# Sharing a pair's moves between ScalarE and GpSimd, and reordering 39 transfers into 30, in a matmul with scale and add

## The chip, the cores and the metric

The kernel runs on one NeuronCore of one Trainium2 chip; the other cores are idle. PE is TensorE (the matmul engine), DVE is VectorE, ACT is ScalarE, POOL is GpSimd and SP is SyncE, which here only issues transfers. SBUF is the memory on the chip that the engines and transfers work on. The metric is the device time of one execution in microseconds (us), median of several; a profiled execution gives the trace. The span of the trace, from the first to the last instruction, is about 1.8 us shorter than the device time.

## The reference

```python
# x: 16 x 512 x 1024, weight: 1024 x 768, add_value: 16 x 512 x 768, all fp32; scale = 0.1
return (scale * np.matmul(x, weight) + add_value).astype(np.float32)
```

The 16 x 512 rows are 64 tiles of 128 rows. Whatever the kernel does, it must read x (33.6 MB), the addend (25.2 MB) and the weight (3.1 MB), and write 25.2 MB: 87.0 MB.

## The kernel before

All transfers are issued by SyncE (SP) in the order of one list. An entry is (what, first tile, number of tiles): x, w for weight, a for addend, o for output, l and r for the two column parts of the last output.

```python
STREAM = [
    ("x", 0, 3), ("w", 0, 2), ("w", 2, 2), ("w", 4, 2), ("x", 3, 1), ("w", 6, 2),
    ("a", 0, 3), ("x", 4, 4), ("a", 3, 1), ("a", 4, 4), ("x", 8, 4), ("x", 12, 4),
    ("x", 16, 4), ("a", 8, 8), ("x", 20, 4), ("x", 24, 8), ("o", 0, 8), ("a", 16, 8),
    ("x", 32, 8), ("a", 24, 8), ("a", 32, 8), ("x", 40, 8), ("o", 8, 8), ("x", 48, 8),
    # ... (15 more, down to)
    ("o", 62, 1), ("l", 63, 1), ("r", 63, 1),
]
X_SLOTS = 16      # x tiles held in SBUF
A_SLOTS = 32      # addend tiles; the output is written over them
MOVED_ACT = [14, 18, 22, ...]     # pairs of tiles moved by ScalarE
MOVED_POOL = [16, 20, 24, ...]    # pairs moved by GpSimd
```

PE needs x transposed and in bf16. The first 14 tiles (and the last four) are cast whole and transposed by PE. The others go in pairs: 16 casting copies of 32 partitions move blocks of a pair from x into a buffer, then VectorE turns 32 x 32 blocks with one stream transpose.

```python
    def move_pair(t0, a):                       # a quarter of the pair's 16 copies
        act = t0 in MOVED_ACT
        # ... (at a == 0: a buffer from a pool of two for ScalarE, of two for GpSimd)
        for b in range(4):
            move = nc.scalar.copy if act else nc.gpsimd.tensor_copy
            move(moved[t0][32 * b:32 * b + 32, :, a, :], src[32 * a:32 * a + 32, :, b, :])

    def turn_moved(t0):
        # ...
        nc.vector.transpose(xt..., moved.pop(t0)...)      # frees the buffer

    def step():                                 # one tile of 128 rows
        t = done["step"]
        for j in range(KJ):                     # 8 parts of K
            if j == KJ // 2:
                # ... transpose(t + 1) on PE if it is no moved tile; casts ahead
                for a in range(4):
                    if in_pair.get(t + 8 - a) == t + 8 - a:
                        move_pair(t + 8 - a, a)
            product(t, j, BOTH)                 # 128x512 and 128x256 matmuls, bf16
        finish(t, BOTH[0], 0, N)                # VectorE: product * scale + addend, over the addend
        if in_pair.get(t + 4) == t + 4:
            turn_moved(t + 4)
```

An x transfer may be issued when the tiles that it overwrites have been cast or moved; an addend transfer when the output that stood there has left; an output transfer when its tiles are finished. Three product buffers (PSUM) stand between PE and VectorE.

## Time and profile before

| | before |
|---|---|
| device time, median of 3 | 210.12 us (210.09 to 210.5) |
| span of the trace | 208.5 us |
| bytes on the one data queue | 87.03 MB, 5,616 packets |
| DMA share from 4 to 204 us | about 1.00, at 428 GB/s |
| PE, ScalarE, GpSimd, VectorE busy | 181.6, 129.0, 124.3, 101.3 us |

The rows are read against each other: no engine is busy all the time, while the 16 DMA rings (one queue, one ring on each of 16 DMA engines) are. The prediction below shows the lines. In a line of a stretch of time, each engine's busy us stands with the number of its instructions in brackets; then come the granted PE clock (1.00 is full), the DMA share and the GB/s moved. The share counts the time in which packets are under way. A transfer ends with 16 landings, one for each ring. The trace records when each came. In the kernel before, the 16 landings of a transfer lie within 0.4 us until 28 us and within 2.4 us at the end.

### The profile page before, as it was taken

The numbers are of one execution on the slowest core, as the hardware profiler recorded it, in microseconds if no ns is written. First come the engines' busy times: TensorE is split into PE (matmuls) and PEld (weight loads), VectorE is DVE, ScalarE is ACT, GpSimd is POOL, SyncE is SP. The second block draws the span as 40 slices with busy tenths as digits, with TensorE's granted clock in tenths as the row PEclk, the third lists the DMA queues.
The fourth block names the chain that finished last, engine by engine and source line by source line (L and its number), as shares of the span: only waits on it lengthen the run. The fifth ranks groups of instructions, "written<-read, shape, count | busy, mean of one in ns | idle before, by whom it ended". The sixth has DMA issues, their size and how long they took to land.

```text
span 208.5 us, 2886 instructions
## 1 busy us (share of the span) xinstructions
PE 181.6 (87%) x1096; PEld 110.7 (53%) x1096; DVE 101.3 (49%) x111; ACT 129.0 (62%) x206; POOL 124.3 (60%) x199
## 2 busy tenths in 40 slices
PE   0599399980899997999999999999999999989960
PEld 0455256650466664566666666666666666656630
DVE  0536535511466514855655555555553685233330
ACT  2423000499959798599999999999999900003210
POOL 1310524379898980999998899999999960001000
PEclk9999889996589999999999999999999999999997
DMA  6999999999999999999999999999999999999995
GB/s 236 415 428 440 413 429 434 421 450 406 454 418 448 407 429 462 404 443 420 442 434 413 461 418 424 420 429 437 421 434 424 432 439 424 429 418 439 429 394 214
DMA packets 5629, 87.21 MB, mean 418 GB/s; under 512 B 624, under 2 KB 752, under 8 KB 2032
## 3 DMA queue, kind: packets, MB, share of 16 engines
q1 hardware_dynamic: 5616, 87.03, 98.2%
q8 instruction: 8, 0.13, 0.3%
q14 instruction: 5, 0.04, 0.0%
HBM read 61.87 MB, written 25.17 MB: 417 GB/s over the span
## 4 chain that ended last, share of the span: by engine, by line
DMA 75%; ACT 9%; PE 7%; DVE 3%; SPq 1%; issue 1%; DVEq 0%
DMA out_dram<-ao 35%; DMA ao<-in_add_value_dram 22%; DMA xs<-in_x_dram 13%; ACT va L118 9%; PE mm L177 6%; DMA ao<-in_weight_dram 5%; DVE ao L185 2%; DVE xt L126 1%; PE tp L156 1%; SPq L258 1%; SPq L99 0%; SPq L264 0%; SPq L272 0%; DVEq L185 0%
## 5 line engine op out<-in xcount | busy, mean ns | idle before, releaser
L177 PE MATMUL mm<-w_bf,xt 128*128 128x256 bf16 (+1 forms) x1024 | 173.8, 331 | 8.8 <-DVE xt L164 6.6
L177 PEld LDWEIGHTS <-xt 128*128 128x128 bf16 x1024 | 101.3, 99 | 76.9 <-DVE xt L164 7.0
L118 ACT CAST va<-xs 32x512 bf16<-32x512 f32 x192 | 118.2, 616 | 28.8 <-DMA xs<-in_x_dram 19.1
L118 POOL CAST va<-xs 32x512 bf16<-32x512 f32 x176 | 106.8, 607 | 15.9 <-DVE xt L126 6.2
L185 DVE SCALAR_TENSOR_TENSOR ao<-mm,ao 128x768 f32<-128x768 f32 (+2 forms) x62 | 58.1, 942 | 78.1 <-PE mm L177 49.1
L146 POOL CAST xb<-xs 128x1024 bf16<-128x1024 f32 x15 | 15.2, 1040 | 43.4 <-PE tp L156 22.5
L164 ACT COPY xt<-tp 128x512 bf16<-128x512 bf16 (+1 forms) x11 | 8.2, 785 | 35.3 <-PE tp L156 35.3
L126 DVE STREAM_TRANSPOSE xt<-va 128x1024 f32<-128x1024 f32 x23 | 28.4, 1234 | 0.0
L156 PE MATMUL tp<-identity,xb 128*128 128x128 f32 x72 | 12.9, 314 | 11.2 <-DVE xb L142 7.4
L156 PEld LDWEIGHTS tp<-identity,xb 128*128 128x128 f32 x72 | 9.8, 161 | 13.7 <-issue 7.6
L164 DVE COPY xt<-tp 128x1024 bf16<-128x1024 bf16 x10 | 6.9, 686 | 10.1 <-PE tp L156 10.1
L101 DVE CAST w_bf<-ao 128x768 bf16<-128x768 f32 x8 | 4.1, 556 | 3.8 <-DMA ao<-in_weight_dram 3.8
L142 DVE CAST xb<-xs 128x512 bf16<-128x512 f32 x3 | 1.9, 696 | 6.8 <-DMA xs<-in_x_dram 6.8
L144 POOL CAST xb<-xs 128x512 bf16<-128x512 f32 x2 | 1.6, 834 | 5.5 <-DMA xs<-in_x_dram 5.5
L144 ACT CAST xb<-xs 128x512 bf16<-128x512 f32 x1 | 0.6, 618 | 4.8 <-DMA xs<-in_x_dram 4.8
L213 DVE TENSOR_SCALAR ao<-mm 128x768 f32<-128x768 f32 x2 | 1.8, 952 | 1.9 <-PE mm L177 1.9
L245 DVE TENSOR_TENSOR ao<-ao 128x768 f32<-128x768 f32 x3 | 2.7, 951 | 0.0
L144 ACT ACT_TABLE_LOAD x1 | 1.3, 1283 | 0.7 <-PEq L289 0.7
L210 ACT ACTIVATE ao<-mm 128x768 f32<-128x768 f32 x1 | 0.8, 817 | 0.0
masks.py:197 POOL MEMSET identity<- 128x128 f32 x1 | 0.2, 204 | 0.3 <-POOLq L289 0.3
masks.py:199 POOL TENSOR_SCALAR_AFFINE_SELECT identity<-identity 128x128 f32<-128x128 f32 x1 | 0.3, 292 | 0.1
L289 POOL MEMSET const-float32-0.0<- 128x1 f32 x1 | 0.1, 98 | 0.2 <-issue 0.2
(3 smaller groups left out, 0.3 us busy)
## 6 DMA issues: line engine op xcount, KB each, us to landing
ao<-in_add_value_dram SPq DMA_DIRECT2D x7, 3072.0 KB, 26.1
out_dram<-ao SPq DMA_DIRECT2D x7, 3072.0 KB, 23.9
xs<-in_x_dram SPq DMA_DIRECT2D x5, 4096.0 KB, 18.8
xs<-in_x_dram SPq DMA_DIRECT2D x5, 2048.0 KB, 26.6
ao<-in_weight_dram SPq DMA_DIRECT2D x4, 768.0 KB, 9.6
xs<-in_x_dram SPq DMA_DIRECT2D x1, 1536.0 KB, 6.1
ao<-in_add_value_dram SPq DMA_DIRECT2D x1, 1536.0 KB, 19.3
out_dram<-ao SPq DMA_DIRECT2D x1, 1536.0 KB, 12.9
```

What stands on the lines that cost most here:

```text
L101: nc.vector.tensor_copy(w_bf[:, j + i, :], ao[:, s + i, :])
L118: move(moved[t0][32 * b:32 * b + 32, :, a, :], src[32 * a:32 * a + 32, :, b, :])
L126: nc.vector.transpose(xt.rearrange("p i c m -> p (i c m)"), moved.pop(t0).bitcast(fp32).rearrange("p c a k -> p (c a k)"))
L142: nc.vector.tensor_copy(xb[:, 0:K // 2], src[:, 0:K // 2])
L144: other(xb[:, K // 2:K], src[:, K // 2:K])
L146: nc.gpsimd.tensor_copy(xb, src)
L156: nc.tensor.transpose(tp[:, c, :], pairs[:, c * P:(c + 1) * P], identity)
L164: evacuate(xt_tiles[t][:, c:c + q, :].bitcast(bf16), tp[:, c:c + q, :].bitcast(bf16))
L177: nc.tensor.matmul(mm_tiles[t, cols[0]][:, n0:n1], lhs(t, j), w_bf[:, j, n0:n1], start=(j == 0), stop=(j == KJ - 1))
L185: nc.vector.scalar_tensor_tensor(a, mm_tiles[t, part][:, n0:n1], float(scale), a, op0=mybir.AluOpType.mult, op1=mybir.AluOpType.add)
L245: nc.vector.tensor_add(ao[:, t, :], ao[:, EARLY_AT + t, :], ao[:, t, :])
L258: nc.sync.dma_start(xs[:, k:k + n, :], rows(x_v, s, n))
```

## The change

The intent: each pair's 16 copies are shared by two engines, so that a pair is ready in half the time; one pool of three buffers serves all pairs; the pairs reach to the last tile; and the transfers become fewer, larger and issued earlier. Cut to its core:

```diff
-    ("x", 0, 3), ("w", 0, 2), ("w", 2, 2), ("w", 4, 2), ("x", 3, 1), ("w", 6, 2),
-    ... 33 more
+    ("x", 0, 3), ("w", 0, 2), ("w", 2, 2), ("x", 3, 1), ("w", 4, 4), ("a", 0, 8),
+    ("x", 4, 4), ("x", 8, 8), ("a", 8, 8), ("x", 16, 8), ("a", 16, 8), ("x", 24, 8),
+    ("a", 24, 8), ("o", 0, 8), ("x", 32, 8), ("o", 8, 8), ("a", 32, 8), ("x", 40, 8),
+    ("o", 16, 8), ("a", 40, 8), ("x", 48, 8), ("o", 24, 8), ("a", 48, 8), ("x", 56, 8),
+    ("o", 32, 8), ("a", 56, 8), ("o", 40, 8), ("o", 48, 8), ("o", 56, 5), ("o", 61, 3),
...
-MOVED_ACT = [14, 18, 22, ..., 58]
-MOVED_POOL = [16, 20, 24, ..., 56]
+MOVED = [14, 16, 18, 20, ..., 60, 62]
...
-    va_pool = ctx.enter_context(tc.tile_pool(name="va_pool", bufs=2))
-    vp_pool = ctx.enter_context(tc.tile_pool(name="vp_pool", bufs=2))
+    va_pool = ctx.enter_context(tc.tile_pool(name="va_pool", bufs=3))
...
         for b in range(4):
-            move = nc.scalar.copy if act else nc.gpsimd.tensor_copy
-            move(moved[t0][32 * b:32 * b + 32, :, a, :], src[32 * a:32 * a + 32, :, b, :])
+            for a, move in ((2 * half, nc.scalar.copy), (2 * half + 1, nc.gpsimd.tensor_copy)):
+                move(moved[t0][32 * b:32 * b + 32, :, a, :],
+                     src[32 * a:32 * a + 32, :, b, :])
...
-                    for a in range(4):
-                        if in_pair.get(t + 8 - a) == t + 8 - a:
-                            move_pair(t + 8 - a, a)
+                    for half in range(2):
+                        if in_pair.get(t + 6 - half) == t + 6 - half:
+                            move_pair(t + 6 - half, half)
```

## The prediction

> **What bounds the kernel now.** I read the page's part 1 first, then part 2, then part 3, then the chain of waits and the stretches at both ends. Part 1 alone would suggest TensorE:
>
> ```profile
> PE 181.6 (87%) x1096; PEld 110.7 (53%) x1096; DVE 101.3 (49%) x111; ACT 129.0 (62%) x206; POOL 124.3 (60%) x199
> ```
>
> Part 2 and part 3 say otherwise:
>
> ```profile
> PE   0599399980899997999999999999999999989960
> ...
> PEclk9999889996589999999999999999999999999997
> DMA  6999999999999999999999999999999999999995
> ...
> DMA packets 5629, 87.21 MB, mean 418 GB/s; under 512 B 624, under 2 KB 752, under 8 KB 2032
> ...
> q1 hardware_dynamic: 5616, 87.03, 98.2%
> ```
>
> The reader is to see that PE has holes (the 0 at slice 10, the 3 and 8 before it) while the DMA row is 9 in every slice but the first and the last. All transfers leave one queue, and its packets fill 98.2% of 16 engines' time: 0.982 x 208.5 = 204.7 us. The chain of waits agrees, 75% DMA:
>
> ```profile
> DMA 75%; ACT 9%; PE 7%; DVE 3%; SPq 1%; issue 1%; DVEq 0%
> ```
>
> The other 25% looks like an invitation to speed up ScalarE, and the waits of the issuing queue do too: its x transfers waited 90.1 us for ScalarE's moves, once for 22.0 us. But a late issue costs only if the queue behind it ran empty. In stretches of 20 us it never did:
>
> ```profile
> core 0: us, PE busy (x) PEld busy (x) DVE busy (x) ACT busy (x) POOL busy (x), PEclk, DMA share, GB/s
> ...
> 44.00:64.00 20.00, 13.43 (x71) 8.12 (x70) 6.92 (x9) 17.59 (x30) 18.03 (x30) 0.74 1.00 428
> ...
> 104.00:124.00 20.00, 20.00 (x125) 12.02 (x123) 11.47 (x12) 19.60 (x33) 18.09 (x30) 1.00 1.01 432
> ```
>
> The first of these holds the worst wait (the x issue at 49.1 us) and a PE idle for some 6 us with a reduced clock, and still the DMA share is 1.00 at 428 GB/s. I check it by counting bytes. An x tile is 0.524 MB; a tile of addend, output or weight is 0.393 MB. By the stream's order 22.02 MB had been issued before that transfer. From 4 to 204 us the rate is 428 GB/s ((87.21 - 0.73 - 0.82) MB in 200 us, the two ends taken from their own stretches), and 0.73 MB had moved by 4 us, so a byte at position B leaves at about 2.3 + B/0.428 us. At 49.1 us some 20 MB were gone: 2 MB, or 4.7 us, were still queued. The tightest wait in the old kernel was hidden, with little to spare.
>
> What is not full is a start of 2.3 us and the end, where the data thin out as the 16 rings finish one after another. Compute ended at 202.04 us, the data at about 207.5 us:
>
> ```profile
> 202.00:204.00 2.00, 0.00 (x0) 0.00 (x0) 0.05 (x1) 0.00 (x0) 0.00 (x0) 1.00 0.96 391
> 204.00:206.00 2.00, 0.00 (x0) 0.00 (x0) 0.00 (x0) 0.00 (x0) 0.00 (x0) 0.90 0.87 342
> 206.00:208.00 2.00, 0.00 (x0) 0.00 (x0) 0.00 (x0) 0.00 (x0) 0.00 (x0) 0.50 0.18 66
> ```
>
> **What the Trainium skill says.** "DMA: Bandwidth & Descriptors", section "Where 436 GB/s comes from", gives 435.2 GB/s as the ceiling of the 16 ports. The trace's 428 to 432 GB/s in full stretches is within 2%, so there is no rate left to win. Its section "Why small descriptors are slow (HBM only)" says that every packet carries a fixed overhead. The packet records of this trace agree that there is one: the median packet took 46 ns for 1,024 B and 1,213 ns for 32,768 B, which is 8.4 ns plus 0.0368 ns a byte; 24,576 B took 912 ns, as that line says. "TensorE: Matmul & The Clock Gate", Part 1, says that an idle window of about 3.4 us halves the PE clock. The trace agrees: PE idle 21.1 to 24.5 us is followed by a clock of 0.50 (26 to 28 us), while the idle 1.2 us near 81 us leaves it at 1.00.
>
> **The change part by part.**
>
> 1. Bytes: none removed. 87.03 MB go through the same queue and rings, 203.3 us at 428 GB/s.
>
> 2. Transfers: 39 become 30. The counts fit one packet per partition row of a transfer and 16 semaphore packets for each transfer: 39 x 144 = 5,616, as part 3 has it. After: 30 x 128, plus 128 because the weight half has two rows a partition, plus 30 x 16 = 4,448. 1,168 packets less at 8.4 ns on 16 rings are 0.6 us. Doing it by size with the medians (before 128 x 46, 128 x 84, 512 x 122, 128 x 159, 512 x 234, 128 x 352, 384 x 461, 640 x 614, 1,792 x 912, 640 x 1,213, semaphores 624 x 9; after 128 x 159, 512 x 234, 128 x 352, 128 x 461, 128 x 574, 128 x 614, 1,920 x 912, 896 x 1,213, 480 x 9) gives 203.2 and 202.4 us of each ring. **Gain on the path: 0.7 us.** It is the only term that I can find there.
>
> 3. The moves. Before, a pair's 16 casts run on one engine: 16 x 0.626 = 10.0 us on ScalarE from first to last, two pairs side by side. After, 8 on each engine: 5.0 us a pair, pairs one after another. Throughput is the same, 2.5 us a tile; latency halves. There are 25 pairs for 23: ScalarE 200 x 0.616 = 123 us, GpSimd 200 x 0.607 plus 11 whole casts of 1.04 and two halves of 0.83, about 134.5 us, both under 203 us. PE loses four tiles' transposes (4 x 0.44 = 1.8 us on its last chain), ScalarE four evacuations of 1.01 us, VectorE gains two transposes of 1.23 us. All of it lies beside the transfers: worth 0.
>
> 4. Issue earlier. Positions in the new queue over 0.428, plus 2.3: x 24-31 starts at 61 us and may be issued when pair 14 is moved and tile 13 is cast, about 51 us; x 32-39 starts at 85 us and needs pair 22 moved, about 75 us (x 16-23 lands near 55 us, then four pairs of 5 us); x 40-47 starts at 110 us, issued at 95; x 48-55 starts at 134 us, issued near 117. Margins of 10 to 17 us in place of under 5. But nothing was lost before, so this saves nothing.
>
> 5. The start. The whole addend 0-7 now stands ahead of x 4-7, which lands near 28 us in place of 23.4. PE idles some 8 us there and restarts at half clock. PE's own work is about 176 us and the addend's arrivals hold it up again later, so this delay is absorbed.
>
> 6. The end. Addend 56-63 has 77.59 MB up to its end in both orders, so it lands as before, near 185.6 us. PE then has tiles 59 to 63 to do (three product buffers, 56 to 58 computed already): 186.7 + 5 x 2.60 = 199.7, last VectorE write about 200.3 us, against 202.04. The last transfer (three tiles) can be issued at 200.4 us and its data begin about 1 us later (the first issue at 0.74 us had data before 2.0 us). The queue reaches it at 2.3 + 85.85/0.428 = 202.9 us. It is hidden by about 1 us.
>
> Sum: 210.1 - 0.7 = **209.4 us**.
>
> **The rivals.** (a) *The earlier issue pays*: if stalls of the issuing queue were real gaps, several us would return, and the 90 us of waits for ScalarE and the 7% of PE in the chain speak for it. Against it is a DMA share of 1.00 in those very stretches. To be over 2% faster, 206 us, the rings would have to move 87 MB at over 434 GB/s; I give it almost nothing. (b) *The last output is exposed*: one transfer of 1.18 MB waits for the last tile where there were five small ones. With PE late by 2 to 3 us (a stall of over 3 us before tile 48, 56 or 59 would halve its clock for some us; I count stalls of 1.4 to 2.6 us there), the margin of 1 us is gone and the time is 210.5 to 212 us. For it: x 56-63 comes 36 us before the end of the data, in place of 51. Against it: moves take half as long, and PE has 1.8 us less to do. (c) *ScalarE and GpSimd in lockstep become the bound*, since each pair now needs both: they give a pair every 5.0 us where PE needs 5.2 us for two tiles. A tie that shows as small PE waits, not as time. (d) *The fewer packets are worth nothing*, because the slowest ring sets the end: the last transfers' landings in the trace spread over 2.4 us between first and last ring. Then 210.1 us stays. The packets taken away are spread evenly over the rings, so I count on most of the 0.7.
>
> **Range and chances.** Expected 209.4. Low, 208.7: packets pay in full, and larger rows close the end more sharply (the last 4 us moved 0.25 MB less than a full rate). High, 210.4: rival (d) plus a little of (b). Faster by over 2% 0.02, within 2% 0.95, slower by over 2% 0.03, which would need a ring run dry or PE half-clocked near the end.
>
> **What would show it right or wrong.** Right: DMA row 9 throughout, the queue's packets 4,448 and about 204 us of ring time, 428 to 432 GB/s in full stretches, waits of x issues for ScalarE or GpSimd still there but no dip after them, the last addend landing near 185.6 us, the last VectorE write near 200, and the span shorter by 0.5 to 1 us. Wrong: a stretch with DMA share well under 1 in the middle (a refused issue), or a last write after 202 us followed by a dip before the last output. The prediction would fail most easily at step 6.

## The result, and the profile after

The changed kernel took **210.1 us** (median of 4, 210.01 to 210.2), the kernel before 210.28 us in the same rounds (median of 4). The ratio is **0.9991** with a 95% interval of 0.9974 to 1.0009. Two later measurements of the same changed kernel gave 1.0011 and 1.0009. There is no change that can be told from noise, where 0.7 us (ratio 0.9967) had been predicted.

The page of the changed kernel, lines that answer to those shown in the prediction:

```profile
PE 177.1 (85%) x1059; PEld 108.4 (52%) x1080; DVE 104.1 (50%) x113; ACT 129.9 (62%) x210; POOL 135.2 (65%) x219
...
PE   0498339999999999999999999999959996799930
...
DMA  6999999999999999999999999999999999999994
...
DMA packets 4461, 87.21 MB, mean 418 GB/s; under 512 B 480, under 2 KB 480, under 8 KB 1120
...
q1 hardware_dynamic: 4448, 87.03, 97.9%
...
DMA 44%; PE 38%; POOL 10%; SPq 1%; issue 1%; DVE 1%; POOLq 0%; DVEq 0%
```

The packets are the 4,448 that were counted beforehand, the rings' time is 0.979 x 208.4 = 204.0 us (before 204.7), and the DMA row has no hole. The chain of waits has changed its face, 38% PE where it was 7%, and the time has not: the chain follows what released each step last, and with a full queue many paths end together. The DMA row, with the GB/s, decides which of them costs.

The issues of four x transfers in the timeline of the changed kernel (start, duration, what):

```profile
54.59 0.33 SPq L250 DMA_DIRECT2D xs<-in_x_dram  x1
...
76.98 0.33 SPq L250 DMA_DIRECT2D xs<-in_x_dram  x1
...
97.91 0.33 SPq L250 DMA_DIRECT2D xs<-in_x_dram  x1
...
118.84 0.33 SPq L250 DMA_DIRECT2D xs<-in_x_dram  x1
```

By the prediction's formula the queue reaches these transfers at 61, 85, 110 and 134 us, so they stood in it 6 to 15 us ahead. The margin is real, and it bought nothing.

The stretches at the end of the changed kernel, with the columns as before:

```profile
202.00:204.00 2.00, 0.00 (x0) 0.00 (x0) 0.00 (x0) 0.00 (x0) 0.00 (x0) 0.95 0.94 401
204.00:206.00 2.00, 0.00 (x0) 0.00 (x0) 0.00 (x0) 0.00 (x0) 0.00 (x0) 0.50 0.68 286
206.00:208.00 2.00, 0.00 (x0) 0.00 (x0) 0.00 (x0) 0.00 (x0) 0.00 (x0) 0.50 0.08 32
```

and VectorE in its timeline, where the fields after the operation are what it waited for:

```profile
185.65 0.96 DVE L178 SCALAR_TENSOR_TENSOR ao<-mm,ao 128x768 f32<-128x768 f32 x1 [2.19 <-DMA ao<-in_add_value_dram]
...
199.86 0.42 DVE L178 SCALAR_TENSOR_TENSOR ao<-mm,ao 128x256 f32<-128x256 f32 x1 [0.18 <-PE mm L170]
```

The last addend is used at 185.65 us as predicted (185.67 before), and the last write ends at 200.28 us (202.04 before). Fewer bytes are left after 204 us than in the kernel before (286 and 32 GB/s in the last two stretches where it had 342 and 66), so most rings do finish sooner. The execution does not.

**The rings.** The landing records of the trace tell why. The table gives, for two transfers that end at the same number of bytes in all of these kernels (output 48 to 55, and the last one), the first ring, the mean and the slowest, in us from the first instruction; the last column is the device time of the same profiled execution. e0, e1 and e11 are repeats; e2, e3 and e4 are told below.

| run | output 48-55: first, mean, slowest | last: first, mean, slowest | device time |
|---|---|---|---|
| before | 197.69, 198.97, 200.12 | 205.17, 206.41, 207.59 | 210.28 |
| before (e0) | 197.96, 199.15, 200.38 | 205.44, 206.62, 207.85 | 210.54 |
| changed | 197.34, 198.76, 200.19 | 204.61, 206.03, 207.46 | 210.20 |
| changed (e1) | 197.52, 198.90, 200.58 | 204.81, 206.19, 207.87 | 210.62 |
| changed (e11) | 197.24, 198.74, 200.16 | 205.56, 206.23, 207.45 | 210.19 |
| e2, packets doubled | 198.83, 200.13, 201.57 | 206.23, 207.51, 208.96 | 211.59 |
| e3, 2 of 8 products | 197.26, 198.10, 200.63 | 204.53, 205.37, 207.92 | 210.67 |
| e4, 1 of 8 products | 197.34, 198.16, 200.68 | 204.65, 205.45, 207.96 | 210.72 |

Two things are to be read. The device time is the slowest landing plus 2.6 to 2.8 us in every row. And the mean ring gains 0.4 us from the change (206.03 against 206.41; 206.19 against 206.62 in the second pair), while the slowest ring gains 0.13 us in one pair and loses 0.02 us in the other. Two traces of one kernel differ in the mean by 0.16 to 0.21 us, so the 0.4 us is clear of that, though not by much. The gain is there, on rings that nobody waits for.

### The profile page after: what moved, and what is told of

Its sections match the earlier page's. It is cut to its first block, busy times and chain, and to the rows that moved or that the text cites. A ratio compares the mean times of both kernels' runs of the same rounds, so it can differ in the third digit from the quotient of the medians.

```text
span 208.4 us, 2843 instructions
## 1 busy us (share of the span) xinstructions
PE 177.1 (85%) x1059; PEld 108.4 (52%) x1080; DVE 104.1 (50%) x113; ACT 129.9 (62%) x210; POOL 135.2 (65%) x219
## 3 DMA queue, kind: packets, MB, share of 16 engines
q1 hardware_dynamic: 4448, 87.03, 97.9%
## 4 chain that ended last, share of the span: by engine, by line
DMA 44%; PE 38%; POOL 10%; SPq 1%; issue 1%; DVE 1%; POOLq 0%; DVEq 0%
PE mm L170 36%; DMA out_dram<-ao 17%; DMA ao<-in_add_value_dram 15%; DMA xs<-in_x_dram 12%; POOL va L110 9%; PE tp L149 2%; DVE ao L178 1%; SPq L93 1%; SPq L250 1%; POOL xb L139 1%; SPq L256 0%; POOLq L139 0%; DVEq L178 0%
## 5 line engine op out<-in xcount | busy, mean ns | idle before, releaser
L170 PE MATMUL mm<-w_bf,xt 128*128 128x512 bf16 (+1 forms) x1003 | 170.6, 327 | 8.3 <-DVE ao L178 6.0
L110 ACT CAST va<-xs 32x512 bf16<-32x512 f32 x200 | 123.2, 616 | 46.0 <-DMA xs<-in_x_dram 43.5
L110 POOL CAST va<-xs 32x512 bf16<-32x512 f32 x200 | 121.7, 608 | 20.8 <-DMA xs<-in_x_dram 11.9
L178 DVE SCALAR_TENSOR_TENSOR ao<-mm,ao 128x768 f32<-128x768 f32 (+2 forms) x62 | 57.2, 935 | 40.3 <-PE mm L170 34.0
L119 DVE STREAM_TRANSPOSE xt<-va 128x1024 f32<-128x1024 f32 x25 | 31.1, 1244 | 29.5 <-POOL va L110 29.0
L139 POOL CAST xb<-xs 128x1024 bf16<-128x1024 f32 x11 | 11.2, 1043 | 29.4 <-DMA xs<-in_x_dram 21.8
L149 PE MATMUL tp<-identity,xb 128*128 128x128 f32 x56 | 10.2, 317 | 14.5 <-DVE xb L135 7.7
L149 PEld LDWEIGHTS tp<-identity,xb 128*128 128x128 f32 x56 | 7.7, 163 | 16.4 <-issue 7.7
L157 ACT COPY xt<-tp 128x512 bf16<-128x512 bf16 (+1 forms) x7 | 4.1, 655 | 9.2 <-PE tp L149 9.2
```

Source lines behind the costliest of these rows:

```text
L119: nc.vector.transpose(xt.rearrange("p i c m -> p (i c m)"), moved.pop(t0).bitcast(fp32).rearrange("p c a k -> p (c a k)"))
L139: nc.gpsimd.tensor_copy(xb, src)
L149: nc.tensor.transpose(tp[:, c, :], pairs[:, c * P:(c + 1) * P], identity)
L157: evacuate(xt_tiles[t][:, c:c + q, :].bitcast(bf16), tp[:, c:c + q, :].bitcast(bf16))
L170: nc.tensor.matmul(mm_tiles[t, cols[0]][:, n0:n1], lhs(t, j), w_bf[:, j, n0:n1], start=(j == 0), stop=(j == KJ - 1))
L178: nc.vector.scalar_tensor_tensor(a, mm_tiles[t, part][:, n0:n1], float(scale), a, op0=mybir.AluOpType.mult, op1=mybir.AluOpType.add)
```

## The experiments

My theory after the result: each packet costs less than its record shows, and of what is gained the slowest ring gets little, because the rings drift apart during the run. The rivals: the packets are free; or compute at the end sets the time after all; or the two halves of the change, moves and list, each have an effect and cancel. Thirteen runs were made, three of them repeats (e0, e1, e11). Each is compared with the kernel before on the same chip in the same rounds.

### e0 and e1: both kernels again

No edit.

> The kernel before, unchanged, timed against itself: what two timings of one program differ by, and a second trace. Both theories: 210.2 us, ratio 1.000. The ring theory (instruction fetches delay single rings, and the slowest ring sets the end): the 16 landings of the last transfer spread over 2.2 to 2.7 us again, with the first jump at the first 16 KB instruction packet. If the spread were chance it would differ by over 0.5 us.

> The changed kernel, unchanged, for a tighter interval and a second trace. Ring theory: the packets saved show in the mean landing of the last transfer (0.4 to 0.7 us under the kernel before), the slowest ring eats a part; 209.9 to 210.1 us, ratio 0.998 to 0.9995. Rival (the packets taken away cost nothing on the rings): mean landing as before, ratio 1.000.

Measured: e0 210.12 us, ratio 0.9995 (0.9979 to 1.0012); e1 210.5 us, ratio 1.0011 (0.9997 to 1.0025). One program differs from itself by about as much as the change does. Of e1's expectation the mean landing came (0.43 us sooner) and the ratio under 0.9995 did not. The spread of the last landings was 2.4 us again in e0 and 3.1 us in e1. In all four traces of the two kernels so far the first wide jump follows the first 16 KB packet of the instruction queue (before: packet at 30.3 us, spread 0.38 us until the transfer that landed at 28 us, 1.71 us in the next).

### e2: the same bytes in twice as many packets

```diff
-            nc.sync.dma_start(xs[:, k:k + n, :], rows(x_v, s, n))
+            for d, e in halves(n):            # (0, n // 2), (n // 2, n)
+                nc.sync.dma_start(xs[:, k + d:k + e, :], rows(x_v, s + d, e - d))
```

and the same for addends and outputs.

> The changed kernel with every x, addend and output transfer cut into two halves issued back to back: 26 transfers more, 26 x 144 = 3,744 packets more, the same bytes. If each packet costs its 8.4 ns on the path: 2.0 us more on every ring, 212.1 us, ratio to the kernel before 1.009. Rival (packets overlap and are free on the path): 210.1 us, ratio 0.999.

Measured: 211.65 us (211.31 to 212.23), ratio 1.0069 (1.0051 to 1.0087). The page of this run:

```profile
DMA packets 8206, 87.22 MB, mean 416 GB/s; under 512 B 896, under 2 KB 896, under 8 KB 2048
```

Against e1 of the same rounds this is 1.15 us more for 3,744 packets. By the landings the mean ring is 1.32 us later, the slowest 1.09 us. So a packet costs a ring 1.32 us x 16 / 3,744 = 5.6 ns, by the device time 4.9 ns, and not the 8.4 ns of its record (against the first trace of the changed kernel it would be 6.3 ns on the mean ring). The records overlap: in this run they sum to 207.0 us a ring (98.4% of 209.8 us, and 0.65 us of instruction packets), but from its first packet at about 1.9 us to its last landing at 207.51 us the mean ring took 205.6 us. That is 1.4 us for 512 packets, 2.7 ns each, and 8.4 less 2.7 is about the 5.6 found. The rival "free" falls, for the slowest ring too. With 5.6 ns the change's 1,168 packets are worth 0.41 us on the mean ring; 0.38 and 0.43 us were measured.

### e3 and e4: a quarter and an eighth of PE's work

Wrong results on purpose: only the first and the last of eight partial products (e3), or the first alone (e4). The transfers are those of the changed kernel.

```diff
     def product(t, j, cols):
+        if 0 < j < KJ - 1:        # e4: if j:
+            return
```

> The changed kernel with only the first and the last of the eight partial products of each tile (wrong result on purpose): a quarter of the PE instructions, so 2 or 3 instruction packets of 16 KB in place of 8, the same transfers. Ring theory: the landings of the last transfer spread over 1.3 us or less and the end comes 0.8 to 1.5 us sooner, 208.6 to 209.3 us. Rival (compute at the end, or the rate alone, sets the time): PE has far less to do, yet if the spread does not come from fetches it stays at 2.4 to 2.9 us and the time at 210.0 to 210.2 us.

> The changed kernel with one of the eight partial products of each tile (wrong result on purpose): PE's program is short enough that I expect none or one 16 KB instruction packet beside the transfers, where the run with two products had 2 and the changed kernel 8. If those packets are what delays the slowest ring: no ring jumps by over 1 us when the first outputs have not begun, the final spread is under 2.2 us, the time 209.3 to 209.8 us. Rival (the slowest ring collects its delay elsewhere too, where output packets begin among the loads): the spread still grows at the first outputs to 2.5 us or more and the time stays at 210.2 to 210.7 us.

Measured: e3 210.64 us, ratio 1.0020 (1.0005 to 1.0034); e4 210.76 us, ratio 1.0029 (1.0012 to 1.0046). Both expectations of a gain failed. Lines of the page of e4:

```profile
PE 62.9 (30%) x183; PEld 25.6 (12%) x184; DVE 100.8 (48%) x113; ACT 129.8 (62%) x210; POOL 134.9 (65%) x219
...
PEclk9996555555555555555555555555555555555555
...
DMA  6999999999999999999999999999999999999992
...
q8 instruction: 1, 0.02, 0.0%
```

PE is busy for 63 us in place of 177 and the kernel is not faster by 0.1 us. This closes the question whether PE's work is on the path: it is not. Nor is the issue of the last output: it came at 198.21 us in place of 200.32 us. It also corrects my idea of the rings. With one instruction packet of 16 KB in place of 8, the mean ring came to 205.45 us, 0.6 to 0.7 us sooner, and the slowest stayed at 207.96 us. In e4 the landings lay within 0.4 us until 54 us; the one packet, at 56.5 us, left one ring 1.3 us behind (spread 1.66 us in the next transfer). Later the spread grew without any such packet: to 2.4 us around the first output transfer (78 us), to 3.2 us by 147 us. So one hit is as good as eight for making a ring late, and other delays add to it. Five instruction packets of 8 KB on another queue (0.31 us each) are a rival that I left untested: one came at 77.15 us, just before the growth at 78 us; but from 88 to 147 us the spread grew by a further 1.0 us and none came. Where the other delays come from, these runs do not settle, nor why they seem to fall on one ring (the slowest landed 0.97 us after the next at 63 us and 1.71 us after it at 81 us).

### e5 and e6: one half of the change each

e5 takes the kernel before with the new list (and the weight loads that go with it). e6 takes the changed kernel with the old list.

```diff
 # e5, against the kernel before
-STREAM = [... 39 entries]
+STREAM = [... the 30 of the change]
 # e6, against the changed kernel
-STREAM = [... 30 entries]
+STREAM = [... the 39 of the kernel before]
```

> The new list of 30 transfers with the old moves. If the transfers carry all that the change does to the rings: mean landing of the last transfer at 206.0 to 206.2 us, as in the changed kernel, slowest ring 1.4 us or more behind the mean, time within 0.3 us of the changed kernel's (ratio to before 0.998 to 1.001). Rival (the shared moves are needed for the early issue, without them the queue runs empty): a dip of the DMA row and 1 us or more on top.

> The shared moves with the old list of 39 transfers. If the moves are beside the path: mean landing 206.4 to 206.6 us as in the kernel before, slowest ring about 1.2 us behind the mean, ratio to before 0.999 to 1.001. Rival (the moves cost something on the path, for GpSimd or ScalarE feed the end later): over 0.5 us slower.

Measured: **e5 216.75 us, ratio 1.0318** (1.0279 to 1.0357); **e6 213.17 us, ratio 1.0146** (1.0105 to 1.0188). Neither half is neutral. Each alone costs what the other one prevents. The times of the two rivals named above for these runs hold. The cause given in e6's rival (the end is fed later) does not: the loss lies in the middle, as the lines below show.

The end of e5, first VectorE and PE in the timeline, then the stretches:

```profile
182.00 1.25 DVE L124 STREAM_TRANSPOSE xt<-va 128x1024 f32<-128x1024 f32 x1 [7.95 <-POOL va L116]
...
184.14 10.94 PE L175 MATMUL mm<-w_bf,xt 128*128 128x512 bf16 x54 [3.28 <-DVE ao L183]
...
208.57 0.42 DVE L183 SCALAR_TENSOR_TENSOR ao<-mm,ao 128x256 f32<-128x256 f32 x1 [0.18 <-PE mm L175]
```

```profile
184.00:188.00 4.00, 3.80 (x16) 1.99 (x17) 2.95 (x4) 0.00 (x0) 1.04 (x2) 0.68 0.99 424
...
196.00:200.00 4.00, 4.00 (x28) 2.47 (x26) 1.06 (x2) 1.58 (x2) 0.69 (x1) 1.00 0.64 276
200.00:204.00 4.00, 3.95 (x27) 2.51 (x27) 1.81 (x2) 1.01 (x1) 0.00 (x0) 1.00 0.59 246
204.00:208.00 4.00, 4.00 (x27) 2.42 (x26) 1.26 (x2) 1.01 (x1) 0.00 (x0) 1.00 0.58 246
```

The new list brings x 56-63 later: used from 171.6 us on. One engine needs 10.4 us for a pair, so VectorE can turn pair 56 only at 182 us; PE had run dry, restarts at a clock of 0.68 in that stretch, and finishes at 209 us, four transposes on the way. From 196 us the DMA share is 0.6: the rings wait for outputs. In the changed kernel VectorE turns the same pair at 176.14 us.

In e6 the old list meets the three shared buffers. A line of its waits, then the same two stretches in the kernel before and in e6, and a part of the second loss alone:

```profile
ACT va L112 <- DVE xt L121: 19.4, 6, 7.0
```

```profile
118.00:122.00 4.00, 4.00 (x27) 2.41 (x25) 3.02 (x3) 3.93 (x7) 3.74 (x7) 1.00 1.01 428
...
138.00:142.00 4.00, 4.00 (x26) 2.45 (x25) 2.22 (x3) 3.92 (x8) 3.74 (x7) 1.00 1.02 434
```

```profile
118.00:122.00 4.00, 3.95 (x26) 2.43 (x26) 2.96 (x3) 3.92 (x7) 3.72 (x7) 1.00 0.81 301
...
138.00:142.00 4.00, 4.00 (x27) 2.38 (x25) 0.00 (x0) 3.92 (x7) 3.72 (x7) 1.00 0.91 375
```

```profile
136.00:138.00 2.00, 1.95 (x13) 1.18 (x13) 1.22 (x2) 1.97 (x4) 1.86 (x4) 1.00 1.10 283
```

ScalarE waited 19.4 us (7.4 us before) for a buffer. With it x 48-55 was issued at 119.66 us, before at 116.08 us. By the prediction's formula some 50.2 MB had moved by then, and 50.33 MB had been issued: the queue was all but empty. By the mean landings, x 48-55 came 1.5 us later than before and everything from the next transfer on 2.5 to 2.8 us later. So the empty queue explains the first 1.5 us. The further 1.1 us went at 136 to 138 us with transfers in the queue (the next output had been issued at 122.59 us): the rate fell to 283 GB/s while the DMA share stayed over 1, for packets of 24,576 B took up to 2.2 us in place of 0.91 us. Why is open. The old list's thin margin is what failed, at x 48-55. The prediction had called x 24-31 the tightest point, with 4.7 us; by the same formula x 48-55 had only 3.8 us in the kernel before (reached at 119.9 us, issued at 116.08 us).

### e8 and e12: shared moves for the last pairs only

e5 with the pairs from 50 on shared and tiles 60 to 63 moved too. In e8 I kept the old order of issue for the quarters of a pair; e12 issues the shared pairs one after another.

```diff
+SHARED = 50
...
+            on_act = a % 2 == 0 if t0 >= SHARED else act
+            move = nc.scalar.copy if on_act else nc.gpsimd.tensor_copy
 # e12 only
-                        if in_pair.get(t + 8 - a) == t + 8 - a:
-                            move_pair(t + 8 - a, a)
+                        t0 = t + 8 - a if t + 8 - a < SHARED else t + 6 - a // 2
+                        ...
+                            move_pair(t0, a)
```

> The new list of transfers with the old moves for pairs 14 to 48 and shared moves for pairs 50 to 62 (60 and 62 moved, not transposed on PE, as in the changed kernel). If the 6 us that the new list alone lost come from the end (10.4 us for a pair's moves after x 56-63 has landed, a halved PE clock, four transposes): last VectorE write back from 209 to 200 or 201 us and the time at 210.2 to 211.2 us, ratio 1.000 to 1.005. Rival (the loss lies in the middle, in late issues at 77 us and after): 214 us or more stays.

> As e8 (new list of transfers, old moves up to pair 48, shared moves from pair 50), but the shared moves issued as in the changed kernel, one pair after another, so that no move of pair 54 stands behind one of pair 56 on ScalarE or GpSimd (in e8 pair 54 waited for x 56-63 that way). If the loss of the new list without shared moves lies at the end: PE reaches tile 56 near 178 us, the last VectorE write comes at 200 to 201.5 us, no dip of the DMA row before 204 us, 210.2 to 211.2 us. Rival (late issues in the middle: the queue ran dry near 77 us): 213 us or more stays.

Measured: e8 213.86 us, ratio 1.0187 (1.0167 to 1.0208), last write 206.70 us; e12 **211.51 us, ratio 1.0057** (1.0020 to 1.0094), last write 202.86 us. Both miss the expected 210.2 to 211.2 us, e12 by 0.3 us. e8 was badly made: an engine takes its instructions in order, and a quarter of pair 56 stood ahead of the rest of pair 54, which so waited for x 56-63. With that mended, 5.3 us of e5's excess over the kernel before (6.6 us, then 1.3 us) are gone: they belonged to the end. Shared moves and the four tiles no longer transposed on PE were changed together, so their shares are not told apart. Two stretches of e12, then the first of them in the changed kernel:

```profile
76.00:80.00 4.00, 4.00 (x25) 2.44 (x25) 2.12 (x3) 3.90 (x8) 3.72 (x7) 1.00 0.97 309
...
204.00:208.00 4.00, 0.00 (x0) 0.00 (x0) 0.00 (x0) 0.00 (x0) 0.00 (x0) 0.80 0.71 298
```

```profile
76.00:80.00 4.00, 4.00 (x26) 2.36 (x25) 3.08 (x3) 3.90 (x8) 3.72 (x7) 1.00 1.04 438
```

The rest, a little over 1 us, is lost at 76 to 80 us, where the rate is 309 GB/s in e5 and e12 alike and 438 GB/s in the changed kernel. The mean landings are level with the changed kernel's up to addend 16-23 and 1.0 us behind from addend 24-31 on. x 24-31 was issued 5 us later here (59.6 us), shortly before the queue reached it. But bytes were still queued at 77 us, so the queue had not run dry. The packets themselves were slow: of the 34 of 24,576 B that began between 76 and 78.5 us in e5, 26 took over 1 us and the longest 2.69 us; in the changed kernel it was 5 of 44, the longest 1.29 us. The DMA share hides this (0.97 at 309 GB/s), the GB/s shows it. I do not know why they were slow. That stays open, here as in e6.

### e9: four buffers for the shared moves, old list

```diff
-    va_pool = ctx.enter_context(tc.tile_pool(name="va_pool", bufs=3))
+    va_pool = ctx.enter_context(tc.tile_pool(name="va_pool", bufs=4))
```

> The shared moves with the old list of transfers and four buffers for moved pairs in place of three. If the 3 us that the moves alone lost come from waiting for a free buffer (19.4 us of ScalarE's waits for VectorE's transposes), so that x 40 to 63 were issued 3 us later than before and the queue ran empty: issues 2 us or more earlier, no dip at 118 to 140 us, 210.2 to 211.0 us. Rival (the moves themselves or GpSimd are too slow for the old list): 212.5 us or more stays.

Measured: **209.87 us, ratio 0.9995** (0.9981 to 1.0008). x 48-55 is issued at 114.52 us, and the stretch at 118 us is full again:

```profile
118.00:122.00 4.00, 4.00 (x26) 2.45 (x25) 2.88 (x3) 3.91 (x8) 3.72 (x7) 1.00 1.05 446
```

So the 3 us of e6, both parts, came from the missing buffer. This is the lowest median of all runs, yet it cannot be told from the kernel before: no version beat either kernel.

### e7 and e10: which rings are late, and taking work off them

e7 cuts the output of tile 61 into pieces of 15, 14, 13, 12, 10, 8, 4 and 52 partitions. e10 cuts the last transfer at partitions 112 and 122.

```diff
-                nc.sync.dma_start(rows(out_v, s, n)[:, :, n0:n1], ao[:, k:k + n, n0:n1])
+                for p0, p1 in PROBES:
+                    nc.sync.dma_start(rows(out_v, s, n)[p0:p1], ao[p0:p1, k:k + n, :])
```

> The changed kernel with the output of tile 61 cut into pieces of 15, 14, 13, 12, 10, 8, 4 and 52 partitions, so that each piece can use only so many rings. A ring that is late at the end should show as one landing far behind the others in each piece that uses it and vanish from the pieces that do not. Ring theory: the transfer before has one or two landings 2.5 us or more behind the first; in the pieces the lag of the slowest changes at one count of rings. If the spread belongs to the end of any transfer and not to rings, every piece shows it alike. The time itself is not compared (1 to 4 us more for the pieces).

> The changed kernel with its last transfer cut at partitions 112 and 122: the pieces of 10 and 6 partitions should use only the low rings, so that rings 10 to 15 carry one row of 9 KB (0.35 us) less and rings 0 to 5 one more. In the probe the slowest ring was 10 or 11 and 12 to 14 came next. If rings set the end and those are late in every run: slowest landing 0.2 to 0.35 us sooner, 209.8 to 210.0 us where the changed kernel beside it has 210.1 to 210.4. Rival (the late ring differs from run to run, or the end is set by the last semaphore alone): no gain, the same time within 0.1 us or up to 0.2 us more for the two small transfers.

Measured in e7 (one look; time 211.96 us, not compared): in the transfer before the pieces the slowest ring landed 2.87 us after the first, the next three 2.31 to 2.36 us. The pieces of 14, 13, 12, 10, 8 and 4 partitions left 15, 14, 13, 11, 9 and 5 landings: one for each partition, and one more that came 0.5 to 1.3 us after the issue. The slowest landing of the pieces of 15, 14, 13 and 12 partitions came at 205.06, 205.23, 205.40 and 205.57 us, 0.17 us later each; in the piece of 10 it came at 204.99 us. So the slowest ring belongs to the two that the piece of 10 no longer uses, if a smaller piece uses some of the rings of the larger one. One ring of the next three was missing with each step from 15 to 12. The spread belongs to rings, not to the end of a transfer. The trace does not number the rings: the numbers in the expectation of e10 are labels, 15 for the ring that the piece of 15 leaves out and so on down.

Measured in e10: 210.27 us, ratio 1.0008 (0.9996 to 1.0021), beside e11 with 210.21 us. In the trace the slowest landing came 6.99 us after that of output 48-55, where the changed kernel has 7.27, 7.29 and 7.29 us: 0.3 us sooner, as computed. But in that execution the slowest ring had been 0.4 us later to begin with (200.58 us against 200.16 in e11), and the device time came 2.86 us after the last landing in place of 2.74 us, with two transfers more. The times show no gain. What one row can shift is smaller than the scatter of the slowest ring.

### e11: the changed kernel a third time

No edit.

> The changed kernel once more, beside the others of this call: a third interval and trace. If the packets are gained on the mean ring and lost on the slowest: ratio to before 0.999 to 1.0015, mean of the last landings near 206.1 us, slowest 1.4 to 1.7 us behind it. Rival (the first two were scatter and 0.4 us are gained): ratio 0.998 or less.

Measured: 210.21 us, ratio 1.0009 (0.9995 to 1.0023). At output 48-55 the slowest ring was 1.42 us behind the mean. At the last transfer it was 1.22 us, with a mean of 206.23 us: here the fastest rings had reached the last output before it was issued and waited about 1 us, the slowest did not.

## Why the prediction was right or wrong

- **What bounds the kernel: right.** The DMA row and the rate are full before and after, and e4 shows it plainly: with 114 us less PE work the time does not fall. Two counts are off. The tightest wait was x 48-55 with 3.8 us, not x 24-31 with 4.7 us (e6). And the 0.25 MB said to be missing in "the last 4 us" is missing from 202 to 206 us; from 204 to 208 us it is 0.9 MB.
- **Step 1, bytes: right.** 87.03 MB in both.
- **Step 2, packets: the step that failed.** "Gain on the path: 0.7 us." The count (4,448) and the ring time (0.7 us less) were exact, but the records' 8.4 ns a packet are not the price. By e2 the price is 5.6 ns on the mean ring, so 0.4 us; 0.38 and 0.43 us were measured. Of these the device time shows nothing: its three ratios are 0.9991, 1.0011 and 1.0009. The time is the slowest landing plus 2.7 us, and in the changed kernel the slowest ring stands 1.42 to 1.68 us behind the mean at output 48-55, in the kernel before 1.15 and 1.23 us. That eats the rest. It is not that packets cost the slowest ring nothing: in e2 it paid 1.09 us of the mean ring's 1.32 us. Whether the larger gap belongs to the change or is scatter is open: it was 0.91 us with the shared moves, old list and four buffers (e9), 1.67 us with three (e6), and 1.07 us with the new list and the old moves (e5), which no simple cause explains.
- **Rival (d), "the fewer packets are worth nothing, because the slowest ring sets the end": this came true in the time.** I had named the 2.4 us spread and set it aside because the packets go evenly over the rings. Even removal does not help when the slowest ring's delay varies by as much as is removed.
- **Step 3, the moves: right in the sum, wrong as a statement on its own.** "All of it lies beside the transfers: worth 0" holds in the pair with the new list. With the old list the three buffers cost 3 us (e6, mended by a fourth buffer in e9), and with the new list the old moves cost 6.6 us (e5).
- **Step 4, earlier issue: right in that nothing was saved.** The x transfers were issued 2 to 4 us later than counted and stood 6 to 15 us ahead, against 10 to 17 predicted. The old margins were not all "under 5": by the formula they were 4.6, 6.9, 6.8, 3.8 and 8.2 us for x 24-31 to x 56-63. That the thinnest had little to spare was shown by e6. The rule behind the step, that a late issue costs only if the queue ran empty, is not shown in full: e5, e8, e12 and e6 each lost about 1 us after late issues with bytes still queued.
- **Step 5, the start: right.** x 4-7 was used at 28.3 us (28 predicted), PE idled 6.5 us ("some 8") and restarted at half clock, and no later loss shows in the time.
- **Step 6, the end: right to 0.1 us.** Addend at 185.65, last write at 200.28 us (185.6 and 200.3 predicted). The hiding is thin, as said: in e11 the fastest rings waited, the slowest not.
- **Rival (b), the exposed last output: did not come in the changed kernel, but e5 is that rival.** What kept it away is what the prediction gave as the argument against it: moves that take half as long and no transposes at the end. e12 puts 5.3 us on the two together.
- **Rival (a) fell** (no gain from earlier issue), **rival (c) fell** (ScalarE and GpSimd in lockstep show as small waits only).

## What to carry to other kernels

When all transfers share one full queue, count for each issue how many bytes stand ahead of it: that margin, not the length of the wait, tells when the queue will run empty. Leave some of it: with margins of 0.2 and 1.5 us (e6, e12) about 1 us more was lost than an empty queue explains. Read the GB/s beside the DMA share, which stays near 1 when packets are slow. Test the halves of a change apart even when the whole is neutral; here +3.2% and +1.5% came to nothing together, because the new list needed the faster moves at the end and the shared moves with three buffers needed the new list's earlier issue. And a saving of some tenths of a microsecond spread over 16 rings is not in the time until the slowest ring has it: look at the last landings, not at the sum.

## What the Trainium skill lacked or had wrong

- "DMA: Bandwidth & Descriptors", section "Why small descriptors are slow (HBM only)", gives the fixed overhead as about 3 cycles a packet. Here the records show 8.4 ns a packet, and the price on a full ring, by doubling the packets, was 5.6 ns on the mean ring and 4.9 ns by the device time. The page has no such price for packets of 4 to 32 KB.
- No page that I read says by how much the 16 rings of one queue drift apart in a long run. Here the landings of one transfer spread from 0.4 to 0.7 us at the start to 2.4 to 3.1 us at 200 us in the two kernels, and the device time is the slowest landing plus 2.6 to 2.9 us.
- "Runtime: NRT & Kernel Launch", section "Instruction fetch mechanics", says that instructions are refilled in 16 KiB blocks and that the cost is mostly hidden. The traces have packets of that size (8 in the kernel, 1 with an eighth of the products). In a kernel that fills its rings they are not hidden from the rings: a block's packet took 0.9 to 1.1 us, and after the single one of e4 one ring was 1.3 us behind.
- The same DMA page, section "Latency and other measured facts", names DMA engines 7 and 15 as the usual slow ones and ties that to transfers issued from GpSimd. Here, with all transfers issued from SP, several rings were late and one of two that a piece of 12 partitions uses and a piece of 10 does not was the latest (2.87 us behind the first).
